# An encoder's first microseconds: longer idle products, first loads on two queues, one-pass bias tables, and mean squares between the last two k steps

## The chip, the cores and the metric

The kernel runs on one core of one Trainium2 chip. The metric is the device time of one execution in microseconds (us). Before the change three runs took 1203.06, 1204.67 and 1206.46 us; their median is 1204.67.

The core has a matrix engine (TensorE, PE in the profile; PEld is its weight load), a vector engine (DVE), a scalar engine (ACT), GpSimd (POOL) and a queue engine (SP) that issues most transfers. Each engine works through its own list of instructions strictly in order, and waits where an operand or a buffer is not ready. Products are summed in PSUM, which has eight banks of 128 x 512 floats; the other engines copy results out from there into SBUF.

## The reference, cut to what matters

The program is a two-layer encoder on 512 tokens of width 1024. What the change touches is the way into layer 0:

```python
hn = rms_norm(h, norm_mix_g[0])            # h = x, 512 x 1024
q, k, v = jnp.split(hn @ w_qkv, 3, axis=-1)
# 16 heads in groups of (window, dilation, heads) = (128,1,6), (512,4,5), (2048,16,5)
logits = einsum(q_blk, k_sel) + rel_bias[t5_bucket(offs)]
p = softmax(logits);  o = p @ v_sel        # then a mixture over the groups, w_o, MLP
```

`rms_norm` divides each token's row by the root of its mean square and multiplies by the gain. The bias comes from a table of 32 buckets x 16 heads, looked up by the distance of two tokens.

## The kernel before, in words

Activations are held transposed: eight tiles `h0` to `h7`, each 128 features x 512 tokens. A product in full float precision is made of three passes over numbers split into a high and a low part (`mm3`, lines 167 to 170): high x high, high x low, low x high. ACT makes the high part by a cast (`whi`, `Ah`), DVE the low part by a subtraction (`wlo`, `Al`). "Product" below means one such pass, 128x128 against 128x512. The gain is multiplied into the split of `h`; the root mean square is a number per token, so it is applied to the result of the product, when that leaves PSUM: `rB` holds it as rows over all partitions, `rBs` the same times -0.125 for q.

Weights come in units of 256 columns (`fetch`, line 146): one 1 MB transfer, then casts and subtractions, two buffers each of `raw`, `whi`, `wlo`. The first two units, q and k of heads 0 to 3, are loaded and split by k step (`load_first`, `split_first`, lines 321 to 332), so that TensorE can begin on the first 128 features while the rest is under way. Four banks (`banks`, line 444: three of the `s` pool and one of `acc`) collect their 2 x 2 column tiles over eight k steps, 12 products each.

Around these steps stand, before the change:

- Idle products (line 130) of the identity with itself, before data is there. The identity is made on POOL.
- Bias tables (`table`, line 381): for each of four blocks of 512 distances one product with the high part and one with the low part of the bias table against a one-hot matrix `ohr` (33 x 2048, loaded by POOL). ACT copies each to `fsb`; after the fourth, `fsb` goes to DRAM (`fd`), and from there windows of it are read back as bias tiles `B0`, `B1`.
- Mean squares (`rstd`, line 247): four one-column products of the sum of squares `nacc` with `ones`; DVE scales, POOL raises to -1/2.
- Rows (`rows`, line 256): four products with the identity that spread the result over the partitions; ACT copies `rB`, DVE makes `rBs`.

The table, the mean squares, the rows and the idle products share a pool of two banks, `t_ps`.

Then the third unit (q of heads 4 to 7; tiles `o_ps` and the second `acc` bank) runs, its results held back; `release` (line 464) multiplies the four first banks by `rB`/`rBs` on DVE. Each q and k tile is then split again for the logits (`split_q`, `split_k`, lines 337 to 354), 12 subtractions on DVE. The fourth unit is k of heads 4 to 7 in two `acc` tiles, `k_703`'s and a second. Logits, softmax and transposes are woven in between.

The kernel's text gives no order by hand for most of this: a scheduler lays each engine's list down from a model of the program's times. `tc.issue_after(x)` adds an edge "in the list after x, if on the same engine", and `tc.high_priority()` favours a block. The banks of a pool are also given out by the scheduler's model, to whichever it takes to be free first.

Of the kernel before, what the change touches and what calls it, by code (L numbers as in the profile page):

```python
# [28 lines left out]
WARM = 7  # L29
# [17 lines left out]
def offset_onehot():  # L47

    oh = np.zeros((33, E_END), np.float32)

    def put(base, rel, valid):
        cols = base + np.arange(len(rel))
        b = t5_bucket(rel)
        oh[b[valid], cols[valid]] = -1.0
        oh[32, cols[~valid]] = 1.0
# [27 lines left out]
def tile_encoder(ctx: ExitStack, tc: tile.TileContext, x, rel_bias, gains, norm_final_g,  # L83
# [33 lines left out]

    ident = const.tile([P, P], F32, name="ident")
    make_identity(nc, ident)
    ones = const.tile([P, 1], F32, name="ones")  # L120
    nc.vector.memset(ones, 1.0)
    warm = const.tile([P, 1], F32, name="warm")
    nc.scalar.activation(warm, ones, AF.Exp)
    mhalf = const.tile([P, 8], F32, name="mhalf")
    nc.vector.memset(mhalf, -0.5)


    idle = t_tile()
    for i in range(WARM):
        nc.tensor.matmul(idle[:, 0:P], ident, ident, start=True, stop=True)  # L130
# [36 lines left out]
    def mm3(ps, ahi, alo, bhi, blo, first, last):  # L167
        nc.tensor.matmul(ps, ahi, bhi, start=first, stop=False)  # L168
        nc.tensor.matmul(ps, ahi, blo, start=False, stop=False)  # L169
        nc.tensor.matmul(ps, alo, bhi, start=False, stop=last)  # L170
# [49 lines left out]
    class Norm:  # L220
# [7 lines left out]
        def feed(self, d, start=False):  # L228
            g = gT[:, self.gcol + d:self.gcol + d + 1]
            if self.xs:  # L230
                xh, xl = self.xs
                nc.scalar.activation(xh[d], hT[d], AF.Copy, scale=g)
# [14 lines left out]
        def rstd(self):  # L247
            ps = t_tile()
            for t in range(NB):
                nc.tensor.matmul(ps[:, t:t + 1], self.acc[:, t * P:(t + 1) * P], ones, start=True, stop=True)  # L250
# [3 lines left out]
            nc.gpsimd.tensor_tensor(self.r, ms, mhalf[:, 0:NB], op=ALU.pow)  # L254

        def rows(self, scaled=None):
            ps = t_tile()
            for t in range(NB):
                nc.tensor.matmul(ps[:, t * P:(t + 1) * P], self.r[:, t:t + 1].broadcast_to([P, P]), ident,
                                 start=True, stop=True)  # L260
            self.rB = rpool.tile([P, SEQ], F32, tag="rB", name="rB")
            nc.scalar.copy(self.rB, ps)
            if scaled is not None:
                self.rBs = rpool.tile([P, SEQ], F32, tag="rBs", name="rBs", bufs=1)
                nc.vector.tensor_scalar(self.rBs, ps, scaled, None, op0=ALU.mult)

# [54 lines left out]
    def load_first(d):  # L321

        nc.sync.dma_start(hT[d], x[d * P:(d + 1) * P, :])
        for src, raw, hi, lo in first:
            nc.sync.dma_start(raw[:, d, :], src[:, d, :])

    def split_first(d):
        norm.feed(d, True)
        for src, raw, hi, lo in first:
            nc.scalar.copy(hi[:, d, :], raw[:, d, :])  # L330
            nc.vector.tensor_sub(lo[:, d, :], raw[:, d, :], f32(hi[:, d, :]))
        norm.square(d, True)
# [37 lines left out]
    tab = stp.tile([33, 16], F32, name="tab")  # L370
    ohr = stp.tile([33, E_END], F32R, name="ohr")
    th = stp.tile([33, 16], F32R, name="th")
    tl = stp.tile([33, 16], F32R, name="tl")
    fsb = stp.tile([16, E_END], F32, name="fsb")

    def load_tables():
        nc.vector.memset(tab[32:33, :], MASKED)
        nc.sync.dma_start(tab[0:32, :], rel_bias)
        nc.gpsimd.dma_start(ohr, onehot)

    def table(c):
        if c == 0:
            nc.vector.tensor_copy(th, tab)
            nc.vector.tensor_sub(tl, tab, f32(th))
        s = slice(c * 512, (c + 1) * 512)
        ps = t_tile()
        nc.tensor.matmul(ps[0:16, :], th, ohr[:, s], start=True, stop=False)
        nc.tensor.matmul(ps[0:16, :], tl, ohr[:, s], start=False, stop=True)
        nc.scalar.copy(fsb[:, s], ps[0:16, :])
        if c == 3:  # L390
            nc.sync.dma_start(fd, fsb)

# [48 lines left out]
    load_tables()  # L441
    for d in range(2, KT):
        load_first(d)
    banks = [s_tile(), s_tile(), s_tile(), acc_tile()]
    for d in range(KT):
        split_first(d)
        for i, ps in enumerate(banks):
            _, _, hi, lo = first[i // 2]
            s = slice((i % 2) * P, (i % 2 + 1) * P)
            mm3(ps, hi[:, d, s], lo[:, d, s], norm.xs[0][d], norm.xs[1][d], d == 0, d == KT - 1)  # L450
        if 2 <= d < 6:
            table(d - 2)
    start.close()
    l0 = ExitStack()
# [14 lines left out]
    run(linear_steps(2, KT, 256, norm.xs, out_q0, bank=lambda: spare_banks.pop()(),  # L469
                     hooks=[(1, release)], hold=held))  # L470
    B1 = l0p.tile([P, 10, P], F32, name="B1", bufs=1)
    PN = [l0p.tile([P, NB, 256], F32, name=f"PN{i}", bufs=1) for i in range(2)]
    for t in PN:
        nc.gpsimd.memset(t[:, 0, 192:256], 0.0)
        nc.gpsimd.memset(t[:, 3, 0:64], 0.0)
# [598 lines left out]
```

## Time and profile before

| | us |
|---|---|
| runs | 1203.06, 1204.67, 1206.46 |
| the profiled execution | 1203.29 |
| its span, first to last instruction | 1201.4 |
| first real product starts | 6.43 |
| first product of the third unit | 35.13 |
| first product of the fourth unit's second tile | 53.06 |
| TensorE's share of the span | 99% |
| mean granted TensorE clock | 0.996 |

In a row of a timeline the first number is the start in us from the span's start, the second the time until the group's end, then engine, line, operation, tile written <- tiles read, shapes, count, and in brackets the idle time before it and what ended it. Products are pipelined: each is shown with about 0.39 us, but at full pace the next one starts after 0.23 us. So the pace is read from the starts.

### The profile page before, as it was taken

What the parts mean: (1) busy time and instruction counts of PE and PEld (TensorE: products, weight loads), DVE (VectorE), ACT (ScalarE), POOL (GpSimd) and SP (SyncE); (2) the same over time, 40 slices, a digit from 0 to 9 for tenths busy, and PEclk for the clock granted to TensorE, in tenths of its full rate; (3) what the DMA queues carried; (4) which work ended last, traced back from release to release, by engine and by line L of the source; (5) the groups of instructions that cost most, each with busy time, mean ns of one, the idle gap of its engine ahead of it and who ended that gap; (6) DMA issues with size and microseconds to landing.
All of it is one profiled execution on the core that took longest, in us unless ns stands there. A gap on an engine that the chain in (4) does not pass through costs nothing.

```text
span 1201.4 us, 14800 instructions
## 1 busy us (share of the span) xinstructions
PE 1186.4 (99%) x5888; PEld 993.0 (83%) x5888; DVE 628.4 (52%) x1056; ACT 500.7 (42%) x924; POOL 81.9 (7%) x141
## 2 busy tenths in 40 slices
PE   8999999999999999999999999999999999999997
PEld 6888877888888888888888898988888888888887
DVE  5875466544433434435458868675644344334323
ACT  6662345433323323314357766665444133223233
POOL 0000000200000000001101121122100000000012
PEclk9999998999999999999999999999999999999999
DMA  7622232333223332333333323312323332333211
GB/s 228 149 76 71 71 93 89 110 97 106 96 79 105 105 100 77 104 105 105 116 105 102 101 82 101 117 51 88 98 80 104 105 105 75 101 105 105 80 62 70
DMA packets 106827, 117.82 MB, mean 98 GB/s; under 512 B 5014, under 2 KB 97366, under 8 KB 106710
## 3 DMA queue, kind: packets, MB, share of 16 engines
q1 hardware_dynamic: 106694, 116.61, 30.7%
q8 instruction: 46, 0.75, 0.3%
q0 software_dynamic: 64, 0.27, 0.1%
q14 instruction: 23, 0.18, 0.0%
HBM read 114.60 MB, written 2.27 MB: 97 GB/s over the span
## 4 chain that ended last, share of the span: by engine, by line
PE 96%; DMA 2%; DVE 1%; issue 1%; ACT 0%; SPq 0%; POOLq 0%; POOL 0%; DVEq 0%; ACTq 0%
PE acc L169 15%; PE acc L170 15%; PE acc L168 15%; PE s_ps L168 14%; PE s_ps L169 14%; PE s_ps L170 14%; PE o_ps L919 2%; PE s_ps L359 1%; PE s_ps L358 1%; PE t_ps L910 1%; PE o_ps L565 1%; PE s_ps L505 0%; PE t_ps L527 0%; DMA fac<-fT 0%; DMA raw<-in_a_w_qkv_dram 0%
## 5 line engine op out<-in xcount | busy, mean ns | idle before, releaser
L157 ACT CAST whi<-raw 128x1024 fp32r<-128x1024 f32 (+1 forms) x196 | 189.1, 1014 | 385.2 <-PE s_ps L169 205.3
L158 DVE TENSOR_TENSOR wlo<-raw,whi 128x1024 fp32r<-128x1024 f32 (+1 forms) x196 | 223.2, 1179 | 41.0 <-ACT whi L157 40.5
L168 PE MATMUL acc<-Ah,whi 128*128 128x512 f32 x472 | 185.6, 393 | 0.0
L170 PE MATMUL acc<-Ah,wlo 128*128 128x512 f32 x472 | 185.3, 393 | 0.0
L169 PE MATMUL acc<-Al,whi 128*128 128x512 f32 x472 | 184.8, 392 | 0.0
L168 PE MATMUL s_ps<-Ah,whi 128*128 128x512 f32 x352 | 137.7, 393 | 0.6 <-ACT whi L330 0.6
L169 PE MATMUL s_ps<-Al,whi 128*128 128x512 f32 x352 | 137.3, 392 | 0.0
L170 PE MATMUL s_ps<-Ah,wlo 128*128 128x512 f32 x352 | 136.6, 391 | 0.0
L169 PEld LDWEIGHTS acc<-Al,whi 128*128 128x128 f32 x472 | 88.8, 188 | 18.2
L170 PEld LDWEIGHTS acc<-Ah,wlo 128*128 128x128 f32 x472 | 88.7, 188 | 18.3
L168 PEld LDWEIGHTS acc<-Ah,whi 128*128 128x128 f32 x472 | 88.9, 188 | 17.7
L713 ACT ACTIVATE u<-u 128x512 f32<-128x512 f32 x64 | 40.0, 628 | 96.6 <-DVE u L712 96.6
L168 PEld LDWEIGHTS s_ps<-Ah,whi 128*128 128x128 f32 x352 | 66.3, 189 | 16.3 <-issue 1.4
L722 DVE TENSOR_TENSOR h<-h,s_ps 128x512 f32<-128x512 f32 x33 | 22.7, 687 | 108.0 <-PE s_ps L170 108.0
L169 PEld LDWEIGHTS s_ps<-Al,whi 128*128 128x128 f32 x352 | 66.5, 189 | 13.8
L170 PEld LDWEIGHTS s_ps<-Ah,wlo 128*128 128x128 f32 x352 | 66.5, 189 | 13.7
L712 DVE SCALAR_TENSOR_TENSOR u<-s_ps,rB 128x512 f32<-128x512 f32 x38 | 26.3, 691 | 76.0 <-PE s_ps L170 73.9
L245 POOL TENSOR_TENSOR nacc<-nacc,nsq 128x512 f32<-128x512 f32 x18 | 25.9, 1439 | 534.7 <-ACT nsq L243 534.3
L168 PE MATMUL s_ps<-Bh,whi 128*128 128x512 f32 x152 | 59.1, 389 | 0.0
L169 PE MATMUL s_ps<-Bl,whi 128*128 128x512 f32 x152 | 59.1, 389 | 0.0
L170 PE MATMUL s_ps<-Bh,wlo 128*128 128x512 f32 x152 | 59.1, 389 | 0.0
L891 DVE CUSTOM_DVE_ANT_0 p<-s_ps,bias 128x512 f32<-128x512 f32 x64 | 43.3, 687 | 25.5 <-PE s_ps L359 17.8
(246 smaller groups left out, 2150.0 us busy)
## 6 DMA issues: line engine op xcount, KB each, us to landing
raw<-in_mlp_w_in_dram SPq DMA_DIRECT2D x32, 1024.0 KB, 5.3
raw<-in_mlp_w_out_dram SPq DMA_DIRECT2D x32, 1024.0 KB, 5.1
raw<-in_b_w_qkv_dram SPq DMA_DIRECT2D x12, 1024.0 KB, 5.1
raw<-in_a_w_qkv_dram SPq DMA_DIRECT2D x10, 1024.0 KB, 8.2
bias<-fd SPq DMA_DIRECT2D x16, 448.0 KB, 3.4
raw<-in_a_w_o_dram SPq DMA_DIRECT2D x4, 1024.0 KB, 5.2
raw<-in_b_w_o_dram SPq DMA_DIRECT2D x4, 1024.0 KB, 5.7
h<-in_x_dram SPq DMA_DIRECT2D x8, 256.0 KB, 4.3
```

Of the source, the lines that this page charges most:

```text
L157: nc.scalar.copy(hi[:, :, c], raw[:, :, c])
L158: nc.vector.tensor_sub(lo[:, :, c], raw[:, :, c], f32(hi[:, :, c]))
L168: nc.tensor.matmul(ps, ahi, bhi, start=first, stop=False)
L169: nc.tensor.matmul(ps, ahi, blo, start=False, stop=False)
L170: nc.tensor.matmul(ps, alo, bhi, start=False, stop=last)
L245: eng.tensor_add(self.acc, self.acc, sq)
L358: nc.tensor.matmul(S, q[m][:, qs], k[m][:, ks], start=True, stop=False)
L712: nc.vector.scalar_tensor_tensor(u, ps, 0.0, nm.rB, op0=ALU.max, op1=ALU.mult)
L713: nc.scalar.activation(u, u, AF.Square)
L722: nc.vector.tensor_add(hT[ct], hT[ct], ps)
L891: nc.vector.tensor_tensor_reduce(out=xt, in0=S, in1=bias[h][m][:, b * P:b * P + SEQ], scale=1.0, scalar=3.0e38, op0=ALU.add, op1=ALU.min, ...
L919: marks["PV"] = nc.tensor.matmul(O[:, b, :], aT[:, k, :], v[:, k, es], start=k == 0, stop=k == NB - 1)
```

## The change

What is changed, part by part:

1. The idle products read a tile that DVE fills with ones (`blank`), and there are twelve of them instead of seven. The column of ones for the mean squares is a column of that tile.
2. The first tile of x is loaded from ACT's queue, the rest from SP's as before. ACT's table load and the small activation that brings it in stand behind that transfer.
3. In the first k step, ACT casts the weights before it squares.
4. The bias tables take one pass: the one-hot matrix has 65 rows, 32 for the high part, 32 for the low, one for masked distances. It is loaded after the fourth k step's cast. Its products stand in pairs behind the seventh and the eighth k step.
5. The mean squares stand between the seventh and the eighth k step, the rows are to be issued in one go behind the last table product.
6. The next weight unit is fetched (in the text of the program) ahead of the rows; casts of later units stand on ACT behind the `rB` copy; POOL's memsets stand behind the power.

```diff
-WARM = 7
+WARM = 12
...
+    blank = const.tile([P, P], F32, name="blank")
+    nc.vector.memset(blank, 1.0)
+    idle = t_tile()
+    for i in range(WARM):
+        nc.tensor.matmul(idle[:, 0:P], blank, blank, start=True, stop=True)
...
     def load_first(d):
-        nc.sync.dma_start(hT[d], x[d * P:(d + 1) * P, :])
+        (nc.sync if d else nc.scalar).dma_start(hT[d], x[d * P:(d + 1) * P, :])
         for src, raw, hi, lo in first:
             nc.sync.dma_start(raw[:, d, :], src[:, d, :])
+        if d == 0:
+            nc.scalar.activation(warm, ones, AF.Exp)
...
     def split_first(d):
         norm.feed(d, True)
+        last = norm.fed
         for src, raw, hi, lo in first:
-            nc.scalar.copy(hi[:, d, :], raw[:, d, :])
+            with nullcontext() if d else tc.issue_after(last.ins):
+                last = nc.scalar.copy(hi[:, d, :], raw[:, d, :])
             nc.vector.tensor_sub(lo[:, d, :], raw[:, d, :], f32(hi[:, d, :]))
-        norm.square(d, True)
+        with nullcontext() if d else tc.issue_after(last.ins):
+            norm.square(d, True)
...
     def table(c):
         if c == 0:
-            nc.vector.tensor_copy(th, tab)
-            nc.vector.tensor_sub(tl, tab, f32(th))
+            nc.vector.tensor_copy(th[0:32], tab[0:32])
+            nc.vector.tensor_copy(th[64:65], tab[64:65])
+            nc.vector.tensor_sub(th[32:64], tab[0:32], f32(th[0:32]))
         s = slice(c * 512, (c + 1) * 512)
         ps = t_tile()
-        nc.tensor.matmul(ps[0:16, :], th, ohr[:, s], start=True, stop=False)
-        nc.tensor.matmul(ps[0:16, :], tl, ohr[:, s], start=False, stop=True)
+        mark = nc.tensor.matmul(ps[0:16, :], th, ohr[:, s], start=True, stop=True)
         nc.scalar.copy(fsb[:, s], ps[0:16, :])
...
+    mark = None
     for d in range(KT):
         split_first(d)
-        for i, ps in enumerate(banks):
-            ...
-        if 2 <= d < 6:
-            table(d - 2)
+        if d == 3:
+            tc.add_manual_dep(read.ins, norm.fed.ins.name, ..., reason="later")
+        if d == KT - 1:
+            with tc.issue_after(mark.ins):
+                mark = norm.rstd()
+        with tc.issue_after(mark.ins) if mark else nullcontext():
+            for i, ps in enumerate(banks):
+                ...
+                end = mm3(ps, ..., d == 0, d == KT - 1)
+        if d >= 6:
+            with tc.issue_after(end.ins):
+                table(2 * d - 12)
+                mark = table(2 * d - 11)
     start.close()
+    fetch()
+    with tc.issue_after(mark.ins), tc.high_priority():
+        mark = norm.rows(-0.125)
...
-    with tc.high_priority():
-        norm.rstd()
-        norm.rows(-0.125)
...
-    run(linear_steps(2, KT, 256, norm.xs, out_q0, ...))
+    with tc.issue_after(norm.copied.ins):
+        run(linear_steps(2, KT, 256, norm.xs, out_q0, ...))
```

The scheduler lays the lists down anew, so instructions move that the diff does not name. Three places, each of before and then of the change.

On TensorE, around the end of the k steps (L250/L251 are the mean squares, L259/L261 the rows, L387/L396 the table products, `nacc` the sum of squares, `o_ps` and the second `acc` the third unit's tiles). Before, the rows between the last k step and the third unit:

```order
L170 MATMUL s_ps<-Ah_126,wlo 128x512
L168 MATMUL acc<-Ah_126,whi 128x512
L169 MATMUL acc<-Al_134,whi 128x512
L170 MATMUL acc<-Ah_126,wlo 128x512
L259 MATMUL t_ps<-ident,rstd 128x128 x4
L168 MATMUL o_ps<-Ah_119,whi 128x512
L169 MATMUL o_ps<-Al_127,whi 128x512
```

With the change, first between the seventh and the eighth k step, then in the third unit:

```order
L171 MATMUL acc<-Ah_129,wlo 128x512
L396 MATMUL t_ps<-ohr,th 16x512 x2
L251 MATMUL t_ps<-blank,nacc 128x1 x4
L169 MATMUL s_ps<-Ah_130,whi 128x512
L170 MATMUL s_ps<-Al_138,whi 128x512
```

```order
L169 MATMUL o_ps<-Ah_129,whi 128x512
L170 MATMUL o_ps<-Al_137,whi 128x512
L261 MATMUL t_ps<-ident,rstd 128x128 x4
L171 MATMUL o_ps<-Ah_129,wlo 128x512
L169 MATMUL o_ps<-Ah_130,whi 128x512
```

The mean squares stood inside the seventh k step and now stand behind the first two table products. The rows stood ahead of the third unit's first product; now they stand behind its 22nd.

On ACT, at the same place (`fsb` are the copies of the tables, `whi` of 128x8x128 the casts of the third and fourth unit). Before:

```order
L402 ACTIVATE lsum<-lsum 128x2
L389 COPY fsb<-t_ps 16x512 x2
L157 CAST whi<-raw 128x8x128 x4
L262 COPY rB<-t_ps 128x512
L350 CAST sp_440<-k_438 64x512
```

With the change:

```order
L397 COPY fsb<-t_ps 16x512 x2
L158 CAST whi<-raw 128x8x128 x2
L397 COPY fsb<-t_ps 16x512 x2
L264 COPY rB<-t_ps 128x512
L158 CAST whi<-raw 128x8x128 x2
L358 CAST sp_441<-k_439 64x512
```

Two table copies and the `rB` copy now stand between the casts of the third and of the fourth unit.

On DVE, from the scaled rows on (`sp` are the splits of q and k, L409/L412/L418/L421/L427 the products with `rB` or `rBs`). Before:

```order
L265 TENSOR_SCALAR rBs<-t_ps 128x512
L418 TENSOR_TENSOR k_438<-s_ps,rB 128x512
L418 TENSOR_TENSOR k_446<-acc,rB 128x512
L409 TENSOR_TENSOR q_410<-s_ps,rBs 128x512
...
L345 TENSOR_TENSOR sp_429<-q_424,sp_427 64x512 x2
L412 TENSOR_TENSOR q_668<-acc,rBs 128x128x4
L158 TENSOR_TENSOR wlo<-raw,whi 128x8x128 x2
L485 ISA xt,mnN<-s_ps,B_369 128x192
```

With the change:

```order
L418 TENSOR_TENSOR q_585<-o_ps,rBs 128x512
L159 TENSOR_TENSOR wlo<-raw,whi 128x8x128 x2
L360 TENSOR_TENSOR sp_441<-k_439,sp_441 64x512
...
L353 TENSOR_TENSOR sp_430<-q_425,sp_428 64x512 x2
L159 TENSOR_TENSOR wlo<-raw,whi 128x8x128 x2
L427 TENSOR_TENSOR k_704<-acc,rB 128x512
L507 ISA xt,mnN<-s_ps,B_396 128x192
```

The second half of four subtractions (`wlo`) moved from ahead of the scaled rows to behind the five products; the fifth unit's pair and the product of the fourth unit's first tile (`k_704`, before `k_703`) now come ahead of the q product, which stands two softmax blocks later. In the built program the fourth unit's second tile had, before, the bank that `q_668` reads out; now it has the bank that `k_704` reads out.

More of the change, by code (lines that the diff above doesn't have):

```diff
@@ L54, in put @@
         oh[b[valid], cols[valid]] = -1.0
-        oh[32, cols[~valid]] = 1.0
+        oh[32 + b[valid], cols[valid]] = -1.0
+        oh[64, cols[~valid]] = 1.0
     d = np.arange(1024) - 512
@@ L115, in wide @@
         return acc_tile() if len(wide_i) % 5 in (0, 2) else s_tile()
+    blank = const.tile([P, P], F32, name="blank")
[3 more added lines that the diff above has]
+        nc.tensor.matmul(idle[:, 0:P], blank, blank, start=True, stop=True)
     ident = const.tile([P, P], F32, name="ident")
     make_identity(nc, ident)
[L120 to L123, printed above, removed]
+    ones = blank[:, 0:1]
     mhalf = const.tile([P, 8], F32, name="mhalf")
     nc.vector.memset(mhalf, -0.5)
-    idle = t_tile()
-    for i in range(WARM):
-        nc.tensor.matmul(idle[:, 0:P], ident, ident, start=True, stop=True)
+    warm = const.tile([P, 1], F32, name="warm")
     hT = [hpool.tile([P, SEQ], F32, tag=f"h{d}", name=f"h{d}") for d in range(KT)]
@@ L169, in mm3 @@
         nc.tensor.matmul(ps, ahi, blo, start=False, stop=False)
-        nc.tensor.matmul(ps, alo, bhi, start=False, stop=last)
+        return nc.tensor.matmul(ps, alo, bhi, start=False, stop=last)
     def linear_steps(ct0, kt, ncol, xs, on_out, bank=None, hooks=(), hold=None, order=None):
@@ L249, in rstd @@
             for t in range(NB):
-                nc.tensor.matmul(ps[:, t:t + 1], self.acc[:, t * P:(t + 1) * P], ones, start=True, stop=True)
+                mark = nc.tensor.matmul(ps[:, t:t + 1], self.acc[:, t * P:(t + 1) * P], ones, start=True, stop=True)
             ms = const.tile([P, NB], F32, tag="ms", name="ms", bufs=2)
@@ L253, in rstd @@
             self.r = const.tile([P, NB], F32, tag="rstd", name="rstd", bufs=2)
-            nc.gpsimd.tensor_tensor(self.r, ms, mhalf[:, 0:NB], op=ALU.pow)
+            self.done = nc.gpsimd.tensor_tensor(self.r, ms, mhalf[:, 0:NB], op=ALU.pow)
+            return mark
         def rows(self, scaled=None):
@@ L258, in rows @@
             for t in range(NB):
-                nc.tensor.matmul(ps[:, t * P:(t + 1) * P], self.r[:, t:t + 1].broadcast_to([P, P]), ident,
-                                 start=True, stop=True)
+                mark = nc.tensor.matmul(ps[:, t * P:(t + 1) * P], self.r[:, t:t + 1].broadcast_to([P, P]), ident,
+                                        start=True, stop=True)
             self.rB = rpool.tile([P, SEQ], F32, tag="rB", name="rB")
-            nc.scalar.copy(self.rB, ps)
+            self.copied = nc.scalar.copy(self.rB, ps)
             if scaled is not None:
@@ L391, in table @@
             nc.sync.dma_start(fd, fsb)
+        return mark
     def lam():
@@ L440, in tile_encoder @@
     load_first(1)
-    load_tables()
+    read = load_tables()
     for d in range(2, KT):
@@ L468, in tile_encoder @@
     spare_banks = [acc_tile, o_tile]
-    run(linear_steps(2, KT, 256, norm.xs, out_q0, bank=lambda: spare_banks.pop()(),
-                     hooks=[(1, release)], hold=held))
+    with tc.issue_after(norm.copied.ins):
+        run(linear_steps(2, KT, 256, norm.xs, out_q0, bank=lambda: spare_banks.pop()(),
+                         hooks=[(1, release)], hold=held))
     B1 = l0p.tile([P, 10, P], F32, name="B1", bufs=1)
     PN = [l0p.tile([P, NB, 256], F32, name=f"PN{i}", bufs=1) for i in range(2)]
-    for t in PN:
-        nc.gpsimd.memset(t[:, 0, 192:256], 0.0)
-        nc.gpsimd.memset(t[:, 3, 0:64], 0.0)
+    with tc.issue_after(norm.done.ins):
+        for t in PN:
+            nc.gpsimd.memset(t[:, 0, 192:256], 0.0)
+            nc.gpsimd.memset(t[:, 3, 0:64], 0.0)
     mnN = l0p.tile([P, NB, 6], F32, name="mnN", bufs=1)
```

24 lines of the change are left out of this document (13 added, 11 removed).

## The prediction

> **What bounds the kernel now.** I read the page's busy shares first, then the table of stages, then the timeline of the stages that the change touches. In the stage table the columns are the stretch, its length, then busy time (and instructions) of PE, PEld, DVE, ACT and POOL, the granted clock, DMA share and GB/s.
>
> ```profile
> PE 1186.4 (99%) x5888; PEld 993.0 (83%) x5888; DVE 628.4 (52%) x1056; ACT 500.7 (42%) x924; POOL 81.9 (7%) x141
> 6.43:10.44 4.01, 4.01 (x10) 3.14 (x10) 3.20 (x9) 3.14 (x7) 0.00 (x0) 1.00 1.01 317
> 36.00:53.06 17.06, 17.06 (x83) 14.27 (x81) 16.74 (x24) 12.02 (x18) 0.00 (x0) 1.00 0.74 154
> 53.06:156.80 103.74, 103.74 (x638) 86.09 (x636) 62.37 (x181) 45.93 (x139) 0.00 (x0) 1.00 0.25 79
> 182.70:196.00 13.30, 11.03 (x59) 8.33 (x60) 12.11 (x16) 9.06 (x13) 0.00 (x0) 0.74 0.46 154
> ```
>
> TensorE is the bound nearly everywhere, and from 53.06 to 156.80 us it has no gap at all: time lost or won before 53.06 is carried to the end. The row to remember is 36.00 to 53.06, where DVE is busy 16.74 of 17.06 us. TensorE does not wait there, but DVE has only 0.3 us to spare.
>
> The start has a second limit, the pace of the array.
>
> ```profile
> 2.48 3.35 PE L130 MATMUL t_ps<-ident 128*128 128x128 f32 x14 [2.48 <-POOL ident masks.py:199]
> 6.43 1.22 PE L168 MATMUL s_ps<-Ah,whi 128*128 128x512 f32 x2 [0.59 <-ACT whi L330]
> 10.01 1.11 PE L170 MATMUL s_ps<-Ah,wlo 128*128 128x512 f32 x3
> 20.01 0.39 PE L170 MATMUL s_ps<-Ah,wlo 128*128 128x512 f32 x1
> 22.73 0.39 PE L170 MATMUL s_ps<-Ah,wlo 128*128 128x512 f32 x1
> ```
>
> From 20.01 to 22.73 there are 12 products, 0.2267 us each: the full pace. The first ten real products take 4.01 us (stage table) where 10 x 0.2267 = 2.27 would do: 1.7 us lost at half pace. The clock column says 1.00 there all the same; later it does show the state:
>
> ```profile
> 179.94 1.09 PE L565 MATMUL o_ps<-pt,vn 128*64 128x128 f32 x16
> 181.37 0.48 PE L169 MATMUL acc<-Al,whi 128*128 128x512 f32 x1
> 185.71 1.11 PE L553 MATMUL t_ps<-ident,v 128*128 128x128 f32 x4 [2.24 <-DVE v L550]
> 191.38 0.44 PE L168 MATMUL s_ps<-oh,whi 128*128 128x512 f32 x1
> 186.00:188.00 2.00, 2.00 (x16) 1.67 (x16) 2.00 (x4) 2.00 (x4) 0.00 (x0) 0.50 0.53 185
> ```
>
> After 2.24 us without work the clock is 0.50 and stays there until 191.38, 5.67 us after work resumed. In that time run 16 value products, 4 transposes and 7 products; the same 16 and 4 took 1.43 us at full pace (179.94 to 181.37) and 7 products take 1.59. So this spell cost 5.67 - 3.02 = 2.65 us. Two prices, then, for a fall to half pace: 1.7 and 2.65 us; full pace returns after 4.0 to 5.7 us of work.
>
> **The head: idle products, first loads, tables.** The idle products no longer wait for the identity on POOL but for one DVE memset.
>
> ```profile
> 0.72 0.20 POOL masks.py:197 MEMSET ident<- 128x128 f32 x1 [0.29 <-POOLq L1064]
> 0.83 0.07 DVE L125 MEMSET mhalf<- 128x8 f32 x1
> 3.92 0.72 ACT L232 ACTIVATE Ah<-h,gT 128x512 fp32r<-128x512 f32 x1 [1.71 <-DMA h<-in_x_dram]
> 5.97 0.74 ACT L330 CAST whi<-raw 128x256 fp32r<-128x256 f32 x2 [0.81 <-DMA raw<-in_a_w_qkv_dram]
> ohr<-in_onehot_dram POOLq DMA_DIRECT2D x1, 264.0 KB, 4.5
> ```
>
> A 128x128 memset on DVE is in no row: between the 0.07 of the small one and the 0.20 of the same size on POOL. I take 0.15, near the row of equal size; TensorE starts at about 1.05 instead of 2.48. Seven products took 3.35 us, 0.479 each, so twelve at half pace end at 1.05 + 5.75 = 6.8. If full pace comes after 4.0 to 5.7 us (at 5.05 to 6.75), the rest of them takes half. Counted as if real work ran at full pace from its start, that start is 5.9 to 6.8; I take 6.4. The loads are ready sooner: h0 (now the ACT queue's first transfer) and the first weights lose the 264 KB in front of them, 0.8 us at the stage table's 317 GB/s, and one issue slot; first casts at about 4.5 instead of 5.97. That gain is hidden behind the idle products. Hidden too: the larger table load (65 rows, some 520 KB, at most twice the 4.5 us) is asked for at the fourth k step and used after the seventh, over 10 us later; and the three small DVE copies of the table, behind which TensorE has 2.7 us of products per step.
>
> The trace of before, charged with the same terms as below (43.9 us of work up to 53.06), has its real work starting at 9.16. So the head gains 9.16 - 6.4 = 2.8 us.
>
> By the Trainium skill, page "TensorE: Matmul & The Clock Gate", section "What's actually happening", the gate decides by free-running windows of 3.4 us; the full pace would then come at 4.5 to 7.9 instead, the start would be 5.6 to 7.3, and the term hardly moves.
>
> ```profile
> 26.92 0.39 PE L170 MATMUL acc<-Ah,wlo 128*128 128x512 f32 x1
> 27.24 0.40 PE L387 MATMUL t_ps<-ohr,th 33*16 33x512 f32 x1
> 27.80 0.50 PE L168 MATMUL s_ps<-Ah,whi 128*128 128x512 f32 x1
> 27.90 0.58 ACT L389 COPY fsb<-t_ps 16x512 f32<-16x512 f32 x1 [2.79 <-PE t_ps L388]
> 29.52 0.39 PE L169 MATMUL s_ps<-Al,whi 128*128 128x512 f32 x1
> 30.55 0.49 PE L170 MATMUL s_ps<-Ah,wlo 128*128 128x512 f32 x1
> 34.10 0.39 PE L170 MATMUL acc<-Ah,wlo 128*128 128x512 f32 x1
> 34.32 1.05 PE L259 MATMUL t_ps<-ident,rstd 128*128 128x128 f32 x8
> 35.13 0.48 PE L168 MATMUL o_ps<-Ah,whi 128*128 128x512 f32 x1
> ```
>
> A pair of table products costs 27.80 - 26.92 - 0.23 = 0.65 us; four pairs become two: 1.3 gained. The mean squares cost 30.55 - 29.52 - 0.23 = 0.80 wherever they stand, the rows 0.80 likewise (34.10 to 35.13). But the mean squares now stand right behind two table products and need the bank of the first, which ACT must copy out first: 0.40 for the product, 0.58 for the copy, two handovers of about 0.05, against 0.56 to when they could have begun: 0.5 us of waiting (0 if the copy were done, 0.75 with slow handovers). The head gains 2.8 + 1.3 - 0.5 = 3.6 us.
>
> **The rows, 22 products later.** This is the step on which the forecast rests. The new order has the rows not at once but behind 22 products of the next unit: they need a bank whose copy to fsb stands on ACT behind the first two weight casts. Everything that frees the first four banks needs the rows, and DVE is what does it.
>
> ```profile
> 36.77 0.58 ACT L262 COPY rB<-t_ps 128x512 f32<-128x512 f32 x1
> 38.61 0.68 DVE L265 TENSOR_SCALAR rBs<-t_ps 128x512 f32<-128x512 f32 x1
> 50.92 1.10 DVE L412 TENSOR_TENSOR q<-acc,rBs 128x512 f32<-128x512 f32 x1
> 51.87 2.33 DVE L158 TENSOR_TENSOR wlo<-raw,whi 128x1024 fp32r<-128x1024 f32 x2
> 56.78 0.69 DVE L418 TENSOR_TENSOR k<-acc,rB 128x512 f32<-128x512 f32 x1
> 50.39 0.28 PE L359 MATMUL s_ps<-sp,sp 128*128 128x256 f32 x1
> 51.44 0.40 PE L170 MATMUL acc<-Ah,wlo 128*128 128x512 f32 x1
> 53.06 0.39 PE L168 MATMUL acc<-Ah,whi 128*128 128x512 f32 x1
> ```
>
> Before, the product at 53.06 (second tile of the fourth unit) needed the q product at 50.92; it was done at 52.02, 1 us early. Now that tile has the bank of the first k tile, so it needs the k product, and DVE's order puts this behind: rBs, five products and twelve splits (18 instructions, 50.92 - 38.61 = 12.31), the wlo pair of the fourth unit (moved in here, 2.33), that of the next (moved ahead, 2.25), and the k product itself (0.69): 17.6 us. DVE can begin only after the rB copy (0.58) and its handovers, 1.0 us behind the rows (0.8 to 1.2), and the release takes 0.15: 18.75 in all. TensorE has meanwhile 50 products (11.33) and 12 logits (nine took 51.44 - 50.39 = 1.05, so 1.4), with switches 12.9. **It then stands still for 18.75 - 12.9 = 5.85 us** (5 to 6.5), and what is queued behind it is all of layer 0. DVE idles some 6 us before the rows and cannot use them: the queue is in order.
>
> In absolute times: start 6.4, 96 products 21.76, two pairs 1.3, mean squares 0.8, waiting 0.5, 22 products 5.0, rows 0.8: rows end at 36.6; the k product releases TensorE at 55.3, against 53.06 before: 2.3 us later (3.6 gained, 5.85 lost).
>
> A stop of 5.85 us is longer than the 2.24 after which the clock fell above, so I add one fall, 1.7 to 2.65: 2.2 us. The same section of the Trainium skill lets the clock fall only after a whole idle window of 3.4 us, which a stop of 5.85 contains in about seven cases of ten (an estimate from that page); the trace differs, it fell after 2.24, and I follow the trace.
>
> Sum: 2.3 + 2.2 = 4.5 us on the profiled execution's 1203.29, or 1207.8. That execution lies 1.38 under the median of the three runs shown; half of this I carry for the parts that the change leaves alone, 0.7: **1208.5 us**.
>
> **Rivals.** (A) The stop comes, but the clock holds: the 2.2 of the fall are not paid, 1207.8 - 2.2 + 0.7 = 1206.3, about no change. For it: the 0.59 us without work at 5.83 and others under 1 us did not bring a fall, so it depends on the time without work and on where it lies; against it, 2.24 us were enough. The rule of the Trainium skill cited above would have it so in three cases of ten. (B) There is no stop: the k product is done when TensorE gets there. Its place is the tile at 53.06, its price all of the 5.85 and the fall; it decides as soon as DVE needs under 12.9 us from the rows on. Then 3.6 us of gain remain: 1203.29 - 3.6 + 0.7 = 1200.4, faster. For it: TensorE has no wait in this stretch today. Against: it needs DVE 5.85 us shorter, and its 16.74 of 17.06 us leave 0.3; the two wlo pairs (4.6 us) are only added. This would also be the case if the rows were in effect issued at once. (C) A second stop, in the exchange of head factors: there TensorE already loses 2.24 us and a fall of clock, and the order of products and transposes ahead of it has changed. One more of the kind costs 2.24 + 2.65 = 4.9: 1213. Against it: the last logits and all that follows them stand as before.
>
> **How the numbers follow.** Forecast 0.50, A 0.16, B 0.22, C 0.12. About 0.3% (3.6 us) is what a measurement of this kernel can tell from no change. Around its value the forecast has 1206.5 to 1210.5 (start 5.9 to 6.8, handovers, the price of the fall), so a little over half of it lies above 1208.3: slower 0.27 + C 0.12 + A 0.03 = 0.42; same 0.23 + A 0.13 + 0.08 of B = 0.44; faster 0.14, the rest of B. The range takes in B's middle and half of C's: 1200.4 to 1212.
>
> **What would show it.** Right: twelve idle products from about 1.05 and no gap before the first real one; full pace by 7; the rows on TensorE at 36 to 37; the first product of the fourth unit's second tile near 55.3 with some 5.8 us idle put down to the DVE k product; matmuls of 0.63 us or a clock of 0.50 behind it. Wrong: that product before 51 us, no wait in it, or DVE's scaled rows earlier than 36 us. A gap before the first real product would break the start, a wait over 1 us at the mean squares the 0.5.

## The result, and the profile after

The kernel became slower by a third of a per cent: 1207.57 us median of 17 runs (1205.26 to 1209.27), against 1203.15 us for the kernel before in 17 runs beside them (1200.78 to 1208.55). The ratio is 1.0033, with a 95% interval of 1.0023 to 1.0044, which does not hold 1, no change. The profiled execution took 1207.57 us with a span of 1205.7; that of before had 1201.4, so these two lie 4.3 us apart. In the experiments one run of e2 (1394.72 us) and one of e9 (1700.77 us) were in a slow state, with a mean granted clock of 0.80 and 0.65, and are left out of every figure.

The timeline of TensorE after the change, at the places that the prediction spoke of (idle products; first real products; tables and mean squares; third unit; rows; the fourth unit's second tile, and where its products get their pace back):

```profile
1.04 4.67 PE L124 MATMUL t_ps<-blank 128*128 128x128 f32 x24 [1.04 <-DVE blank L121]
5.46 0.95 PE L169 MATMUL s_ps<-Ah,whi 128*128 128x512 f32 x3
8.30 0.62 PE L169 MATMUL s_ps<-Ah,whi 128*128 128x512 f32 x2
...
24.62 0.62 PE L396 MATMUL t_ps<-ohr,th 65*16 65x512 f32 x2
25.67 1.05 PE L251 MATMUL t_ps<-blank,nacc 128*128 128x1 f32 x8 [0.43 <-ACT fsb L397]
29.89 0.40 PE L169 MATMUL o_ps<-Ah,whi 128*128 128x512 f32 x1
34.89 1.05 PE L261 MATMUL t_ps<-ident,rstd 128*128 128x128 f32 x8
48.61 0.28 PE L367 MATMUL s_ps<-sp,sp 128*128 128x256 f32 x1
54.08 0.80 PE L169 MATMUL acc<-Ah,whi 128*128 128x512 f32 x1 [5.19 <-DVE k L427]
55.10 0.63 PE L171 MATMUL acc<-Ah,wlo 128*128 128x512 f32 x1
59.34 0.40 PE L169 MATMUL acc<-Ah,whi 128*128 128x512 f32 x1
```

The start is early and without a gap, the third unit begins at 29.89 instead of 35.13, and then TensorE stands for 5.19 us at the fourth unit's second tile, released by DVE's k product. Behind the stop the next twelve products take 59.34 - 54.08 = 5.26 us where 2.72 would do. DVE, in the same stretch, waits 5.08 us for the rows and then has no gap until the k product:

```profile
36.60 0.69 DVE L267 TENSOR_SCALAR rBs<-t_ps 128x512 f32<-128x512 f32 x1 [5.08 <-ACT rB L264]
40.19 2.35 DVE L159 TENSOR_TENSOR wlo<-raw,whi 128x1024 fp32r<-128x1024 f32 x2
49.64 1.39 DVE L353 TENSOR_TENSOR sp<-q,sp 64x512 fp32r<-64x512 f32 x2
51.06 2.36 DVE L159 TENSOR_TENSOR wlo<-raw,whi 128x1024 fp32r<-128x1024 f32 x2
53.34 0.69 DVE L427 TENSOR_TENSOR k<-acc,rB 128x512 f32<-128x512 f32 x1
```

The stage table shows the granted clock behind the stop (columns as in the prediction). The second row lies wholly in the stop, which runs from 48.89 to 54.08; the third and fourth hold the slow products:

```profile
45.64:49.05 3.41, 3.25 (x20) 2.68 (x18) 3.31 (x6) 3.09 (x5) 0.00 (x0) 1.00 0.66 147
49.05:52.46 3.41, 0.00 (x0) 0.00 (x0) 3.35 (x5) 0.56 (x1) 0.00 (x0) 1.00 0.69 146
52.46:55.87 3.41, 1.79 (x4) 1.50 (x5) 3.41 (x10) 1.56 (x5) 0.00 (x0) 0.50 0.59 79
55.87:59.28 3.41, 3.41 (x9) 2.67 (x8) 2.91 (x11) 1.80 (x7) 0.00 (x0) 0.50 0.98 327
```

### The profile page after: what moved, and what is told of

The parts are those of the page before. It is cut to its first block, busy times and chain, and to the rows that moved or that the text cites. A ratio compares the mean times of both kernels' runs of the same rounds, so it can differ in the third digit from the quotient of the medians.

```text
span 1205.7 us, 14814 instructions
## 1 busy us (share of the span) xinstructions
PE 1186.7 (98%) x5894; PEld 995.2 (83%) x5894; DVE 629.0 (52%) x1057; ACT 500.6 (42%) x924; POOL 82.4 (7%) x141
## 3 DMA queue, kind: packets, MB, share of 16 engines
HBM read 114.86 MB, written 2.27 MB: 97 GB/s over the span
## 4 chain that ended last, share of the span: by engine, by line
PE 94%; DVE 1%; DMA 1%; ACT 1%; issue 1%; SPq 0%; POOLq 0%; POOL 0%; DVEq 0%; ACTq 0%
PE acc L169 14%; PE acc L170 14%; PE acc L171 14%; PE s_ps L171 14%; PE s_ps L170 14%; PE s_ps L169 14%; PE o_ps L941 2%; PE s_ps L366 1%; PE s_ps L367 1%; PE t_ps L932 1%; PE o_ps L587 1%; PE s_ps L527 0%; PE t_ps L549 0%; DMA fac<-fT 0%; PE t_ps L124 0%
## 5 line engine op out<-in xcount | busy, mean ns | idle before, releaser
L171 PEld LDWEIGHTS acc<-Ah,wlo 128*128 128x128 f32 x472 | 89.3, 189 | 18.4
```

The source lines that it names most:

```text
L171: return nc.tensor.matmul(ps, alo, bhi, start=False, stop=last)
```

## The experiments

All ratios below are to the kernel before, run beside on the same chip. Its median was 1203.14 us beside e1 to e4, 1202.58 beside e5 to e8 and 1202.48 beside e9 to e12, so medians of different groups can be off by some 0.7 us against each other. "Changed kernel" is the kernel after the change (1.0033).

| run | what | us, median | ratio, 95% interval |
|---|---|---|---|
| e1 | changed, rows directly behind the tables | 1200.37 | 0.9973, 0.9958 to 0.9987 |
| e2 | changed, fifth unit's weights behind the k product | 1203.70 | 1.0003, 0.9988 to 1.0019 |
| e3 | changed, stop filled with idle products | 1204.61 | 1.0013, 0.9999 to 1.0027 |
| e4 | before, idle products in the exchange of factors | 1201.98 | 0.9990, 0.9975 to 1.0006 |
| e5 | before, with the new start alone | 1201.55 | 0.9990, 0.9981 to 0.9998 |
| e6 | before, with one-pass tables alone | 1204.07 | 1.0014, 1.0005 to 1.0023 |
| e7 | changed, 7 idle products | 1208.61 | 1.0045, 1.0033 to 1.0057 |
| e8 | changed, 18 idle products | 1206.56 | 1.0037, 1.0023 to 1.0050 |
| e9 | changed, rows behind six products | 1202.49 | 0.9996, 0.9983 to 1.0009 |
| e10 | e9 with idle products in the exchange | 1201.10 | 0.9990, 0.9979 to 1.0001 |
| e11 | changed, tables loaded early | 1209.83 | 1.0057, 1.0036 to 1.0077 |
| e12 | e2 with 8 idle products in its stop | 1202.05 | 0.9995, 0.9981 to 1.0009 |

### What the stop is made of: e1, e2, e9

**e1** holds the third unit's products behind the rows. The lists of ACT stay as in the changed kernel; on DVE the fifth unit's pair of subtractions is now parted by the q product.

```diff
-    with tc.issue_after(norm.copied.ins):
+    with tc.issue_after(norm.copied.ins), tc.issue_after(mark.ins):
         run(linear_steps(2, KT, 256, norm.xs, out_q0, ...))
```

> The changed kernel, with the third unit's products held behind the rows, so that the rows stand directly behind the last table products. Theory (DVE starts late because the rows stand 22 products deep in the third unit, and its queue then reaches the bank's product 18.4 us after the rows): TensorE waits about 0.6 us at the rows for a bank, the rows end near 31.3 instead of 35.7, DVE's scaled rows start near 32, the fourth unit's second tile is released before TensorE gets there (about 48.9 against 49.7), no stop and no fall of the clock; 4.3 us of delay and 2.5 us of slow products go, 1207.6 - 6.8 = about 1200.8, a ratio to before of 0.998. Rival 1 (the length of the queue alone, with the two moved subtractions of weights, makes the stop): a stop of at least 2 us stays and 1204 to 1207 results. Rival 2 (a stop moves on to another wait): no stop at this tile, but a new one of several us behind it, 1204 to 1208.

Measured 1200.37, a gain over the kernel before. TensorE's rows in its profile, and the q product on DVE that now frees the bank:

```profile
31.54 1.13 PE L261 MATMUL t_ps<-ident,rstd 128*128 128x128 f32 x8 [0.65 <-ACT fsb L397]
49.92 0.39 PE L170 MATMUL acc<-Al,whi 128*128 128x512 f32 x1
50.15 0.39 PE L171 MATMUL acc<-Ah,wlo 128*128 128x512 f32 x1
50.37 0.39 PE L169 MATMUL acc<-Ah,whi 128*128 128x512 f32 x1
```

```profile
47.91 1.23 DVE L159 TENSOR_TENSOR wlo<-raw,whi 128x1024 fp32r<-128x1024 f32 x1
49.05 1.10 DVE L421 TENSOR_TENSOR q<-acc,rBs 128x512 f32<-128x512 f32 x1
```

The wait at the rows is the 0.65 us that was expected, and the products of the fourth unit follow each other at 0.23 us with no stop. Neither rival came: nothing took the stop's place. But e1 changes two things, since the scheduler also gave this tile the bank that the q product frees. With the bank and the list of the changed kernel, the release would stand 18.38 us behind the rows' end as it did there, at 32.42 + 18.38 = 50.8, an estimate from the two profiles, and TensorE is there at 50.37. So nearly all of the 5.19 us goes with the place of the rows, and some 0.4 with the bank and the parted pair.

**e2** leaves the rows where they are and shortens DVE's queue by the fifth unit's pair.

```diff
+    def out_k4(ct, ps):
+        out_k0(ct, ps)
+        if ct == 2:
+            with tc.issue_after(kprod[-1].ins):
+                fetch()
-    run(linear_steps(2, KT, 256, norm.xs, out_k0))
+    run(linear_steps(2, KT, 256, norm.xs, out_k4, ahead=False))
```

> The changed kernel, with the fifth unit's load, casts and subtractions put behind the k product of the fourth unit's first tile; nothing else moves ahead of it. Theory (the stop is the length of DVE's queue from the rows on): the queue loses the pair of 2.36 us, the release comes at about 51.7 instead of 54.08, the stop shrinks from 5.19 to about 2.8 us; it is still longer than the 2.24 us after which the clock fell elsewhere, so the slow products stay: 1207.6 - 2.4 = 1205.2. If the clock holds after 2.8 us: 1202.7. Rival (the tile waits for the bank or its weights, whatever DVE has queued): the stop keeps its 5.2 us, 1207.6.

```profile
51.90 0.50 PE L170 MATMUL acc<-Ah,whi 128*128 128x512 f32 x1 [2.92 <-DVE k L430]
52.73 0.63 PE L170 MATMUL acc<-Ah,whi 128*128 128x512 f32 x1
```

The stop shrank from 5.19 to 2.92, by 2.27 us for a pair of 2.36: the queue is what TensorE waits for, and the rival falls. A fall of the clock is still there (0.43 us from product to product, from 52.6 to 56.0). The time came out 1.5 us better than expected: up to 173.5 us the profile is 2.45 us ahead of the changed kernel's, as expected; another 2.1 us come in the exchange of head factors, for the reason told in the last section.

**e9** puts the rows behind six products of the third unit, so that these cover the 0.65 us.

```diff
+    with tc.issue_after(mark.ins):
+        next(third)
+        next(third)
+    with tc.issue_after(prod[-1].ins), tc.high_priority():
+        mark = norm.rows(-0.125)
+    with tc.issue_after(norm.copied.ins):
+        fetch()
+    with tc.issue_after(mark.ins):
+        run(third)
```

> The changed kernel, with the rows behind the first six products of the third unit instead of 22, and the fourth unit's load, casts and subtractions behind them. Theory: in the run with the rows directly behind the tables TensorE waited 0.65 us there for a table's copy; here the third unit's first products cover that wait, the rows end near 32, and there is still no stop at the fourth unit's second tile: 0.6 us better than that run, 1200.4 - 0.6 = 1199.8. Rival (DVE is late again, or the third unit's weights are): a stop of 1 us or more and 1201 to 1204.

It gave 1202.49, no gain: the rival's case.

```profile
48.81 2.36 DVE L159 TENSOR_TENSOR wlo<-raw,whi 128x1024 fp32r<-128x1024 f32 x2
51.09 1.02 DVE L422 TENSOR_TENSOR q<-acc,rBs 128x512 f32<-128x512 f32 x1
```

```profile
32.53 1.05 PE L262 MATMUL t_ps<-ident,rstd 128*128 128x128 f32 x8
52.26 0.47 PE L170 MATMUL acc<-Ah,whi 128*128 128x512 f32 x1 [2.17 <-DVE q L422]
```

The 0.65 us were covered, but DVE's scaled rows came 0.91 us later than in e1 (34.23 against 33.32), and the list had the whole fifth pair ahead of the q product, not half of it: that product begins 2.04 us later than in e1 (51.09 against 49.05), and TensorE stands for 2.17 us. In e1 the q product ended at 50.15 and the tile's first product began at 50.37, so e1 had only some 0.2 us to spare, and one subtraction on DVE decides.

### The slow products behind the stop: e3, e12, e4, e10

**e3** fills the stop with 22 idle products, in a bank that is free then.

```diff
+    def filler():
+        t = o_tile()
+        with tc.high_priority(), tc.issue_after(prod[-1].ins):
+            for i in range(22):
+                nc.tensor.matmul(t[:, 0:P], blank, blank, start=True, stop=True)
-    run(linear_steps(2, KT, 256, norm.xs, out_k0))
+    run(linear_steps(2, KT, 256, norm.xs, out_k0, hooks=[(KT, filler)]))
```

> The changed kernel, with 22 idle products (about 4.4 us at full pace) put into the stop, behind the last product of the fourth unit's first tile, in a bank that nobody uses then. They compute nothing. Theory (the slow products behind the stop come from time without work on TensorE): the second tile still starts at about 54.1, but its products run 0.23 us apart from the start; 2.5 us gained, 1207.6 - 2.5 = 1205.1. Rival (the slow products come from what runs beside them, DVE at 4.70 of 5.26 us and transfers at 0.84 of the queues): no change, 1207.6.

```profile
47.69 5.08 PE L636 MATMUL o_ps<-blank 128*128 128x128 f32 x44
54.59 0.50 PE L169 MATMUL acc<-Ah,whi 128*128 128x512 f32 x1 [0.40 <-DVE k L427]
55.17 0.40 PE L171 MATMUL acc<-Ah,wlo 128*128 128x512 f32 x1
55.41 0.40 PE L169 MATMUL acc<-Ah,whi 128*128 128x512 f32 x1
```

The tile is released 18.4 us behind the rows as before (they are 0.5 us later in this execution), and the products behind it run at 0.23 to 0.24 us although DVE and the transfers do the same work beside them. 1204.61 is 3.0 us under the changed kernel (2.4 by the two ratios to before, whose intervals just overlap), for 2.5 expected. The profile is clear: the slow products come from the idle time, not from what runs beside them.

**e12** puts 8 such products (1.6 us) into e2's stop.

```diff
-            for i in range(22):
+            for i in range(8):
```

> The changed kernel, with the fifth unit's weights behind the k product (as in the run with a stop of 2.92 us) and eight idle products, 1.6 us, in the stop that is left. Theory (a fall needs over half of a stretch of 3.41 us without work): about 1.3 us without work stay, less than 1.7, so no fall whatever the place in the grid; the release is not earlier, the 8 products that ran 0.2 us late each run at full pace: 1204.0 - 1.7 = 1202.3. Rival (any stop over 1 us brings the fall): 1204.0.

It gave 1202.05, with 1.26 us of waiting left and a clock of 1.00 from 40 to 66 us: the clock held, as expected. The time alone would not show it, since the intervals of e2 and e12 overlap.

**e4** does the same to the kernel before, in the exchange of head factors.

```diff
             T = t_tile()
+            if ct == 7:
+                with tc.high_priority(), tc.issue_after(prod[-1].ins):
+                    for i in range(10):
+                        nc.tensor.matmul(T[:, 0:P], ident, ident, start=True, stop=True)
```

> The kernel before, with ten idle products (2.0 us) put into the exchange of head factors, between the last products of the values and the two products ahead of the 2.24 us wait. They compute nothing. Theory (time without work makes the clock fall): the wait shrinks to 1.2 us or so, the clock column stays at 1.00 from 185.7 on and the 2.65 us of slow products go: 1203.2 - 2.6 = 1200.6, ratio 0.998. Rival (the fall there has another cause, such as the transfers and casts of that stage): clock 0.50 as before, 1203.2.

The stage from 184 to 196 us, of the kernel before and then of e4:

```profile
184.00:196.00 12.00, 10.29 (x57) 8.03 (x58) 11.49 (x16) 9.06 (x13) 0.00 (x0) 0.72 0.44 148
```

```profile
184.00:196.00 12.00, 10.06 (x64) 7.16 (x65) 12.00 (x15) 9.86 (x13) 0.00 (x0) 1.00 0.43 144
```

The clock did not fall, as the theory had it, but the 2.65 us did not follow: 1201.98 is 1.2 us better, with an interval that holds no change. DVE is busy for all of the 12 us there. At full clock TensorE is idle for 1.94 us there, against 1.71 before: it now waits for DVE, which at half clock the slow products had hidden. That this is what took back the rest of the 2.65 us is argued from the two rows, not tested.

**e10** adds the same idle products to e9, with e4's diff (`blank` in place of `ident`).

> The kernel with the rows behind six products of the third unit, and ten idle products in the exchange of head factors as in the run on the kernel before. Theory (TensorE falls to half pace at the end of a stretch of 3.41 us, on a grid that goes on through the whole run, in which it was idle for over half the time): the fall at the exchange goes, worth 1.2 to 1.7 us: 1199.8 - 1.5 = 1198.3, ratio 0.996, the fastest of all. Rival (the stage hangs on DVE and transfers, busy without a gap from 184 to 196 us in the run on the kernel before): at most 0.5 us, 1199.3 to 1199.8.

The fall at the exchange is gone (clock 1.00 from 170 to 200 us). 1201.10 is 1.4 us under e9 and inside the theory's 1.2 to 1.7, though the two intervals overlap; 1198.3 was not reached, because e9 lay 2.7 us above its own expectation. It is not faster than e1.

### The start: e5, e11, e6, e7, e8

**e5** takes only the start of the change (idle products, first tile on ACT's queue, casts ahead of the square); from the diff shown with the change.

```diff
-WARM = 7
+WARM = 12
...
-        nc.sync.dma_start(hT[d], x[d * P:(d + 1) * P, :])
+        (nc.sync if d else nc.scalar).dma_start(hT[d], x[d * P:(d + 1) * P, :])
```

> The kernel before, with the start of the change alone: twelve idle products on a tile that DVE sets, the first tile of x on the ACT queue, casts ahead of the square in the first k step. Tables, mean squares and rows as before. Theory (the head gains by its start alone, and what follows is only shifted): first real product at about 5.5 instead of 6.43, at full pace, which is worth 9.16 - 5.6 = 3.5 us; the fourth unit's second tile starts without a stop; 1203.2 - 3.5 = 1199.7, ratio 0.997. Rival 1 (the earlier start runs into DVE, which had 0.3 us to spare between 36 and 53 us): a stop of 1 to 3 us at that tile, 1200.5 to 1203. Rival 2 (the lost 1.7 us at half pace were no half pace but late data): only the 1 us of the earlier start, 1202.2.

1201.55 is 1.0 us better, not 3.5. The ACT rows of its first microseconds show why:

```profile
4.50 0.39 ACT L333 CAST whi<-raw 128x256 fp32r<-128x256 f32 x1
7.32 0.40 ACT L333 CAST whi<-raw 128x256 fp32r<-128x256 f32 x1 [2.43 <-DMA raw<-in_a_w_qkv_dram]
```

The second unit's first weights arrive at 7.3 us, and TensorE waits for them in the middle of the first k step. No stop comes at the fourth unit (rival 1), and the half pace is gone from the first products (0.23 to 0.32 us from one to the next); in its place the data is late. The time is near rival 2's, but the half pace had been one.

Not every execution of the kernel before has that half pace, however. e4 has the lists of the kernel before, on TensorE, ACT, DVE and POOL, up to 33 us, and its rows start 1.36 us earlier than the 34.32 of the profile of before:

```profile
32.96 1.05 PE L259 MATMUL t_ps<-ident,rstd 128*128 128x128 f32 x8
```

Its first real product starts later (6.97 against 6.43), but at full pace: the trace's list of clock changes begins with a rise to full clock at 6.14 us, that of before at 10.55. In e5 the rows start at 33.23, no earlier than in e4. So the 3.5 us expected of the start, with 1.7 of half pace in them, were read from one slow start.

**e11** is the changed kernel without the edge that holds the table load back until the fourth k step.

```diff
-        if d == 3:
-            tc.add_manual_dep(read.ins, norm.fed.ins.name, ..., reason="later")
```

> The changed kernel, with the one-hot matrix of the tables (520 KB) loaded at the start, behind the loads of the second k step, instead of after the fourth k step's cast. Theory (the late table load is what lets the start be early): the first weights are cast at about 7.3 to 7.6 us as in the runs of the start alone and of the tables alone, instead of 4.55; the first real product comes at 7 to 8 instead of 5.46, TensorE waits again in the first k step, and rows, stop and all behind are 1.5 to 2.5 us later: 1209 to 1210. Rival (the twelve idle products or the first tile's queue set the start, and the table load only fills gaps): 1207.6.

```profile
4.52 0.39 ACT L337 CAST whi<-raw 128x256 fp32r<-128x256 f32 x1
8.89 0.40 ACT L337 CAST whi<-raw 128x256 fp32r<-128x256 f32 x1 [3.98 <-DMA raw<-in_a_w_qkv_dram]
```

1209.83, 2.3 us above the changed kernel's median (2.9 by the ratios) and in the expected range, though the two intervals overlap; in the profile the stop ends 3.15 us later (57.23 against 54.08). Only one half of the first weights is late, by more than expected (8.89); the other is cast at 4.52. In the changed kernel both are cast from 4.55 on. So by the profiles the late table load is a large part of the early start; with the table load in front, the twelve idle products and the second queue brought 1 us in e5.

**e6** gives the kernel before the one-pass tables, loaded at the start.

```diff
-    ohr = stp.tile([33, E_END], F32R, name="ohr")
+    ohr = stp.tile([65, E_END], F32R, name="ohr")
...
-        nc.tensor.matmul(ps[0:16, :], th, ohr[:, s], start=True, stop=False)
-        nc.tensor.matmul(ps[0:16, :], tl, ohr[:, s], start=False, stop=True)
+        mark = nc.tensor.matmul(ps[0:16, :], th, ohr[:, s], start=True, stop=True)
```

> The kernel before, with the one-pass tables alone, in four places of the k steps as the order lays them. Theory: four products of about 0.3 us less, 1.3 us, minus what the larger table load (520 instead of 264 KB) costs at the start, where it stands in front of later weights: 0.8 us at 317 GB/s if it delays them, hidden by TensorE's backlog if not; 1202 to 1202.7. Rival (the larger load starves the second and third k step): slower than before by up to 1 us.

1204.07, slower than before by 0.14%: the rival's case. The 520 KB delay the first weights:

```profile
7.55 0.71 ACT L331 CAST whi<-raw 128x256 fp32r<-128x256 f32 x2 [2.32 <-DMA raw<-in_a_w_qkv_dram]
```

The cast stood at 5.97 before. That its rows nevertheless come 0.86 us earlier in the profile (33.46 against 34.32) does not show in the median of the runs: the profile of before has the slow start told under e5, and the profiled execution of e6 (1202.57 us) is the second fastest of its eleven. Against e4's rows (32.96) those of e6 are 0.5 us late.

**e7** and **e8** change only the count of idle products.

```diff
-WARM = 12
+WARM = 7        (e7; 18 in e8)
```

> The changed kernel with seven idle products as before instead of twelve. Theory (full pace needs 4.0 to 5.7 us of work, whatever the work is): the idle products end at about 1.04 + 2.8 = 3.9, the first real product waits for its weights' cast until about 5.1, and the array has worked 2.8 us only before, with a gap behind; so the first real products run at half pace for 1.5 to 3 us; loss 1 us or more, which the stop behind does not give back, since it hangs on the rows: 1208.6 to 1209.6. Rival (the data's arrival at 5.4 us sets the start, the idle products don't matter): 1207.6.

> The changed kernel with eighteen idle products instead of twelve. Theory: twelve already end where the first weights are cast (5.46 us); six more cost 0.2 to 0.4 us each at the start, 1.2 to 2 us, and everything behind is shifted by that: about 1209. Rival (in these microseconds something else is late, so that more idle products are hidden): 1207.6.

Neither can be told from twelve: their intervals overlap that of the changed kernel. In e7's profile the first real product starts at 4.94 and the next ones follow 0.23 to 0.33 us apart: the expected half pace of 1.5 to 3 us was not there. But full clock came at 4.67 us in this execution, and at 6.90 in that of e9, with twelve idle products; so one profile does not show that seven are enough in every execution. In e8's the start is 1.7 us later, as expected, and the stop too (55.77, again 5.19 us), but the exchange of head factors gives it all back: 803.00 there for the product that the changed kernel has at 803.80.

## Why the prediction came out right, step by step

- **The stop.** Right in place, releaser and cause. Its terms: rows end 35.70 (36.6 forecast), from there to the release 18.38 us (18.75), TensorE's work in between 13.19 (12.9), stop 5.19 (5.85). e1 took the late rows away and the stop went (the last 0.4 us of it by the bank), e2 shortened the queue and the stop shrank by as much.
- **The fall of the clock.** Right: granted 0.50 from 52.46 to 59.3, 2.54 us lost (2.2 forecast). e3 shows that it is the idle time. The upper price of 2.65 us counted seven products in the trace of before; it has six from 188.66 to 190.96, so that fall cost 5.67 - 1.43 - 1.36 = 2.88.
- **The head.** Under-sized. Counted at full pace the real work starts at 8.30 - 12 x 0.2267 = 5.58, not 6.4; the idle products took 4.42 us, since full pace came back at 4.68, after 3.6 us of work instead of the 4.0 to 5.7 assumed. A pair of tables cost 0.46 instead of 0.65; the wait at the mean squares was 0.43 (0.5). At the third unit's start the gain is 35.13 - 29.89 - 0.81 for the rows = 4.4 us (3.6). This is the gain between two profiles. The 9.16 that the forecast started from holds the 1.7 us of half pace that e4, with the same lists, did not have: against e4, whose third unit begins at 33.77, the gain is 33.77 - 29.89 - 0.81 = 3.1. Which start an execution gets is luck, and the forecast was built on a slow one.
- **The loads.** The first casts were forecast at about 4.5 and came at 4.55, for 5.97 before. The 0.8 us put on the 264 KB in front of them is too small a price for a table load at the start: in e5 (264 KB) and e11 (520 KB) ACT waited 2.43 and 3.98 us for the second half of the first weights. The sum was not hurt, because the change does put that load off.
- **The sum.** 54.08 against 53.06 is 1.0 us late (2.3 forecast), plus 2.54 for the fall; another 0.7 us was lost between 59 us and the end, which no step had: 0.5 of it up to 176 us (0.2 of this is a longer wait of TensorE for DVE there), 0.2 in the exchange; not traced further. 4.28 in all, for 4.5. Part of the agreement is luck: the rows' end was put 0.9 too late and the way from there to the release 0.37 too long, which made the forecast 1.3 us too slow at the second tile; 0.34 more for the fall and the missing 0.7 brought it back.
- **The 0.7 us for the median** was wrong: over 17 runs the kernel before has a median of 1203.15, and its profiled execution with 1203.29 lay in the middle, not low. Without it the forecast would have been 1207.8.
- **Rivals.** B's price, 1200.4 "if the rows were in effect issued at once", is what e1 measured: 1200.37; but the 0.7 us for the median is in that price, and over the kernel before beside it e1 gained 2.8 us, not 3.6. A (the clock holds) is e3, 1204.6; its 1206.3 was too high because the tile came 1.3 us sooner than forecast and 0.7 had been added for the median. C did not come: 2.38 us at the exchange instead of 2.24.

## What to carry to other kernels

An engine with a queue in order and 0.3 us to spare must get its first input on time: look up which instruction starts it, and follow that through every list when a change moves things, banks and tile copies included. Here the start gained 4.4 us in the profiles, and 22 products ahead of four small ones, with two pairs of subtractions put in front of the product that frees the bank, took it back and 3.6 us more. Count a stop twice, once for its length and once for the pace behind it, and compare profiles stage by stage: later stages absorb or add a microsecond or two by themselves, and so does the start.

## What the runs showed of the hardware

**The clock falls on a grid.** In the changed kernel's profile the clock falls at 52.46 and at 189.00 and comes back at 59.3 and 195.8. 189.00 - 52.46 = 136.54 = 40 x 3.4135, and the returns stand two such steps behind the falls. The same holds inside each of the other profiles with several changes. Stretches of 3.41 us laid on this grid show what decides. Of the changed kernel, and then of e9 and of e10:

```profile
175.35:178.76 3.41, 2.10 (x24) 1.72 (x25) 1.48 (x4) 1.09 (x3) 0.00 (x0) 1.00 0.99 313
185.59:189.00 3.41, 1.27 (x5) 0.40 (x3) 1.49 (x4) 1.83 (x4) 0.00 (x0) 1.00 0.69 203
189.00:192.41 3.41, 2.52 (x18) 2.19 (x20) 3.41 (x5) 3.31 (x5) 0.00 (x0) 0.50 0.54 169
192.41:195.83 3.42, 3.42 (x13) 2.54 (x10) 3.42 (x5) 2.88 (x4) 0.00 (x0) 0.50 0.00 0
```

```profile
47.86:51.27 3.41, 2.23 (x15) 1.75 (x13) 3.37 (x5) 1.24 (x2) 0.00 (x0) 1.00 0.78 169
51.27:54.68 3.41, 2.42 (x11) 2.05 (x12) 3.37 (x12) 1.97 (x8) 0.00 (x0) 1.00 0.79 94
```

```profile
48.95:52.36 3.41, 1.24 (x6) 1.02 (x6) 3.41 (x12) 1.55 (x6) 0.00 (x0) 1.00 0.79 156
52.36:55.77 3.41, 3.41 (x9) 2.68 (x9) 3.13 (x8) 2.40 (x9) 0.00 (x0) 0.50 0.89 167
```

In the changed kernel, 1.31 of 3.41 us idle (38%): no fall. 2.14 idle (63%): the next stretch is at half clock; that one has 0.89 idle (26%), and the one behind it is at half clock too; it has none, and full clock returns. Over all fourteen profiles, stretches at full clock with 55% idle or more were followed by a fall, and those with 49% or less were not; of five with 52 or 53%, three were (before, e2, e8) and two were not (e4, e11). So the bound lies near a half, and the busy column does not place it more exactly. At half clock, a stretch with 12% idle or less was followed by full clock, one with 20% or more by another at half. The same stop of 2.17 us brought no fall in e9, where the grid cut it into 1.18 and 0.99, and a fall in e10, where one stretch held all of it: a stop under 3.4 us is a matter of the grid's place, which differs from execution to execution.

The first rise to full clock lies on the same grid. The clock column shows 1.00 ahead of it because the trace's list of changes begins with that rise. In the eleven profiles whose idle products start at 1.04 us it came between 4.57 and 6.90 us; in the three where they start at 2.48 or 2.49, at 5.73, 6.14 and 10.55. So what a start costs also differs from execution to execution.

The Trainium skill, page "TensorE: Matmul & The Clock Gate", section "What's actually happening", has the window of 3413 ns and that it runs freely; both agree (3.4135 us above). It lets the clock fall after an idle window and does not say how idle; here half sufficed. What the prediction took from the trace, that 2.24 us of waiting can be enough, holds only with the 0.65 us shortly before: the stretch that ended at 184.63 in the profile of before held these and 1.16 of the 2.24, 53% together.

**The exchange of head factors absorbs it.** From the small transposes at 171 to 179 us to the product near 800 us the same work took 625.4 to 625.7 us in the profiles of e2, e3, e5 and e8, where the fall came early in that stage, ahead of a wait that is set by DVE and transfers; 627.6 to 628.1 in before, changed, e7 and e9, where it came behind that wait and lasted two stretches; and 626.3 to 627.0 in the six others, where it lasted one stretch or did not come. So one profile can lie 2.8 us from another in a stage that only e4 and e10 touched, as much as several of the edits here were worth.
